# One decoder step: T4's second-level forms from resident parts, the early pairs' sums on VectorE, and block 0 of the hidden layer loaded before its use

## The chip, the cores and the metric

The kernel runs on one core of a Trainium2 chip. The metric is device time in microseconds (us) of that core; lower is better. TensorE (PE in the profile) multiplies matrices, with its weight loads in a row of their own (PEld). VectorE (DVE), ScalarE (ACT) and GpSimd (POOL) do elementwise work, and SyncE (SP) issues most DMAs. Each engine works through its own queue in order; semaphores hold an instruction until what it needs is done.

## The reference, cut to what matters

The program is one layer of a hybrid decoder for 1024 prompt tokens and 8 sample tokens that share the weights: three token mixers (a gated convolution, a state-space scan, cross-attention), their merge, and a SwiGLU feed-forward layer with norms. The change lies in the feed-forward part:

```python
def swiglu(xn, w_gate, w_up, w_down):
    return (jax.nn.silu(xn @ w_gate) * (xn @ w_up)) @ w_down
...
xp = xp + swiglu(rmsnorm(xp, norm_ffn_w[l]), w_ffn_gate[l], w_ffn_up[l], w_ffn_down[l])
```

`xn` has 1032 rows (1024 + 8) of 1024 elements; the hidden size is 2816, that is, 22 blocks of 128.

## The kernel before

**Number format.** Products are made in three passes: every operand is split into a high part (a rounded copy, a cast on ScalarE) and a low part (source minus high part, on VectorE), and hi x hi, hi x lo and lo x hi are summed in PSUM. So every new operand costs one ScalarE and one VectorE instruction ahead of TensorE. `form` (L402, L404) does this for activations, `st_split` (L258, L259) and `w_half` (L2049, L2050) for weights.

**Gate and up projections.** The hidden blocks are worked on in pairs, in the list `pairs`: (0, 9), then eight pairs whose blocks lie four apart, then (10, 19) and (20, 21); n counts them from 0 to 10. For each pair the gate ("g") and then the up ("u") projection is one Strassen product of a 2 x 2 block matrix: seven products of half size with combinations of the activations, the forms B11, T1, nT2, B21, T3, B22 and T4 (names as in `NAMES`), each with its hi and lo part resident. T4's eight parts live in the four tiles of the pool tag `ring`. A name such as u2m or g4c in the profile is the PSUM tile of that projection and block.

For n = 0 to 3, `strassen` runs with the products of B11 and B21 already made (`st_early`); they are fetched from DRAM (`e_d`). Five products are left. Before them, `st_sums` and `st_adds2` combine the two blocks of weights: three sums by `plus` (L296, 128 x 512 each) and one scaled difference (L309) on VectorE. `plus` runs on the engine in `adder`: VectorE at first, GpSimd from n = 1. The first sum is issued behind the instruction in `freed[0]`, where that is on the same engine. VectorE evicts PSUM at L380, L381 (which sets `freed[0]`), L390, L392 and L397, and ScalarE copies at L344 and L379. TensorE accumulates into the same two PSUM tiles again, so it waits for those evictions. The SwiGLU products of a pair follow at L2202 to L2218.

For n = 4 to 10, `chain` makes five of the seven products, and the two others are split once more by a second level of Strassen, `leaf`, whose seven products are interleaved with the next pair's chain: leaf l = 0 for B21 and l = 1 for T4. Pair 4's chain has no leaf work beside it. `leaf_begin` loads and sums a leaf's weights into two `ev` tiles.

**Second-level forms.** `leaf_forms(l)` returns eight functions: `fetch` gets the source (four blocks, two tiles), the others make one second-level form each (four of them with a combination on VectorE at L2024, L2028, L2032 or L2036), split it (L2018 cast, L2019 difference) and store five of the seven through the single tile of the pool tag `stage` into `lf_d`; the last two stay resident. The sources B21 and T4 are stored in `lr_d` when their forms are made (L1862, L1967) and read back by `fetch` (L2008) into two of the five `ev` tiles. Both sets are put into the list `pend` at n = 1; `tick()`, called three times in each early `strassen`, takes one entry. `flush()` empties the list after pair 3. Then `ring_load` begins to bring the stored forms into the four `ring` tiles.

**Down projection.** Part 0 has block 0 by itself and the eight blocks of `PARTS[0]`; the second part has blocks 9 and 10 and eight more. For a block by itself `hidden` loads the SwiGLU result from `h_d` into an `ev` tile and splits it. The 16 halves `pd` (L2337) are its products with the weights; for part 0 the last two leaves (names l010 and l110) are interleaved with the first eight. `hidden_forms` loads the stored combinations of the eight blocks from `hf_d` into `ev` tiles and splits them (names B1100 to T402), and `down_pairs` runs Strassen products d00, d02, d04, d06 with them. In part 0 the first three forms are issued before the `pd` loop, the fourth behind the fourth copy of `pd` results and the others behind the eighth. `begun` prepares the first weights of d00.

**What sets the order.** The code is written once in program order; a scheduler places instructions into each engine's queue by priority in program order and by when it expects operands and buffers to be ready. Where an instruction waits longer on the chip than expected, everything behind it on its queue waits too. `tc.issue_after(x)` puts the instructions of a block that run on x's engine behind x. Pools hold a fixed number of tiles for a tag: 5 `ev`, 8 `big`, 3 raw weight tiles, 12 + 12 for forms, 4 `ring`, 1 `stage`; a load waits until a tile is free.

Of the kernel before, what the change touches and what calls it, by code (L numbers as in the profile page):

```python
# [9 lines left out]
F32 = mybir.dt.float32  # L10
F32R = mybir.dt.float32r
AF = mybir.ActivationFunctionType
ALU = mybir.AluOpType
# [4 lines left out]
P = 128  # L18
# [25 lines left out]
def tile_kernel(ctx: ExitStack, tc, a, o):  # L44
# [3 lines left out]
    def f32(t):  # L48
        return t.bitcast(F32)
# [21 lines left out]
    def dram(name, shape):  # L71
        return dp.tile(shape, F32, tag=name, name=name)
# [100 lines left out]
    def ev_tile(name, shape=(P, TT + 4), dt=F32):  # L173
        return ev.tile(list(shape), dt, tag="ev", name=name)
# [16 lines left out]
    def flush():  # L191
        while pend:
            tick()
# [42 lines left out]
    def b3(t, n):  # L236
        return t.rearrange("p (a b) -> p a b", a=n)
# [181 lines left out]
    h_d = dram("h_d", [NF, P, TT])  # L419
    hf_d = dram("hf_d", [7, 8, P, HT])  # L420
    e_d = dram("e_d", [7, P, TT])
    lr_d = dram("lr_d", [2, 4, P, HT])
    lf_d = dram("lf_d", [2, 5, P, 4, HC])
    q_d = dram("q_d", [8, P, TT])
    k_d = dram("k_d", [2, P, D])
# [1433 lines left out]

    def form_second(kt):  # L1860
        b21 = normed(kt + 4, 0)
        SY.dma_start(lr_d[0, kt], b21)  # L1862
        form("B21", kt, b21)

    for half in range(2):
# [97 lines left out]
    def last_forms():  # L1963
        for kt in range(4):
            t2, b21 = x2[kt][:, HS[0]], x2[kt + 4][:, HS[0]]
            V.scalar_tensor_tensor(t2, t2, -1.0, b21, op0=ALU.mult, op1=ALU.subtract)
            SY.dma_start(lr_d[1, kt], t2)  # L1967
            form("T4", kt, t2, freed[0])

    def hidden_pair(nm, j, j2):  # L1970
# [30 lines left out]
    def leaf_forms(l):  # L2001
        xy = []

        def fetch():
            for i in range(2):
                t = ev_tile(f"lr{l}{i}")
                xy.append(t[:, :TT].rearrange("p (k h c) -> p k h c", k=2, h=2))
                SY.dma_start(b3(t[:, :TT], 2), lr_d[l, 2 * i : 2 * i + 2].rearrange("k p c -> p k c"))  # L2008

        def b(i, j):  # L2010
            return xy[i - 1][:, :, j - 1, :]

        def put(i, src):
            if i < 5:
                t = pstg.tile([P, 4, HC], F32R, tag="stage", name=f"lf{l}{i}")
            else:
                t = leaf_tiles[l, i] = act_tile(("ah", "al")[i % 2], f"lf{l}{i}", shape=(P, 4, HC))
            S.copy(t[:, 0:2, :], src)  # L2018
            V.tensor_sub(t[:, 2:4, :], src, f32(t)[:, 0:2, :])  # L2019
            if i < 5:  # L2020
                SY.dma_start(lf_d[l, i], f32(t))

        def t1():
            V.tensor_sub(b(1, 1), b(1, 2), b(1, 1))  # L2024
            put(1, b(1, 1))

        def t2():
            V.tensor_sub(b(1, 1), b(1, 1), b(2, 2))  # L2028
            put(2, b(1, 1))

        def t3():
            V.tensor_sub(b(1, 2), b(2, 2), b(1, 2))  # L2032
            put(4, b(1, 2))

        def t4():
            V.scalar_tensor_tensor(b(1, 1), b(1, 1), -1.0, b(2, 1), op0=ALU.mult, op1=ALU.subtract)  # L2036
            put(6, b(1, 1))

        return [
            fetch, lambda: put(0, b(1, 1)), t1, t2, lambda: put(3, b(2, 1)), t3, lambda: put(5, b(2, 2)), t4,  # L2040
        ]

# [153 lines left out]

    for n, (j, j2) in enumerate(pairs[:4]):
        if n == 1:
            adder[0] = G
            pend.extend(leaf_forms(0) + leaf_forms(1))  # L2200
        s1, s2, pa = hidden_pair("g", j, j2)
        S.activation(s1, s1, AF.Silu)  # L2202
        S.activation(s2[:, HS[1]], s2[:, HS[1]], AF.Silu)
        S.activation(s2[:, HS[0]], pa, AF.Silu, scale=-1.0)
        u1, u2, pa = hidden_pair("u", j, j2)
        V.tensor_mul(s1, s1, u1)
        V.tensor_mul(s2[:, HS[1]], s2[:, HS[1]], u2[:, HS[1]])
        V.scalar_tensor_tensor(s2[:, HS[0]], pa, -1.0, s2[:, HS[0]], op0=ALU.mult, op1=ALU.mult)
        if j2 != j + 4:
            SY.dma_start(h_d[j], s1)  # L2210
            SY.dma_start(h_d[j2], s2)
            continue
        (b11, b12), (b21, b22) = ([t[:, c] for c in HS] for t in (s1, s2))
        (t1, t3_), (t2, t4) = ([t[:, c] for c in HS] for t in (u1, u2))
        V.tensor_sub(t1, b12, b11)
        V.tensor_sub(t2, t1, b22)
        V.tensor_sub(t3_, b22, b12)
        V.scalar_tensor_tensor(t4, t2, -1.0, b21, op0=ALU.mult, op1=ALU.subtract)  # L2218
        for f, t in enumerate((b11, t1, t2, b21, t3_, b22, t4)):
            store_pair(n, f, t)  # L2220
    flush()
    for _ in range(4):
        ring_load()

# [3 lines left out]
    def leaf_next():  # L2228
        l, n, og, ou, after = jobs.popleft()
        return leaf(l, n, ready.popleft(), og, ou, after)  # L2230

    for n in range(4, len(pairs)):
        j, j2 = pairs[n]
        tiles = []
        for i, nm in enumerate("gu"):
            oo = [big(f"{nm}{j}o{h}") for h in (1, 2)]
            tiles += oo
            side = leaf_next() if n > 4 else iter(())
            for step, _ in enumerate(
                chain(2 * (n - 4) + i, *(wblock(ffn[nm], x * P) for x in (j, j2)), f"{nm}{j}", oo)  # L2240
            ):
                next(side, None)
                if step == 2 and (n > 4 or i):
                    ready.append(leaf_begin(0, n) if i else leaf_begin(1, n - 1))
            for _ in side:
                pass
            s2, u2 = tiles[1], oo[1]
            if i == 0:
                S.activation(s2[:, HS[1]], s2[:, HS[1]], AF.Silu)
            else:  # L2250
                V.tensor_mul(s2[:, HS[1]], s2[:, HS[1]], u2[:, HS[1]])
        s1, s2, u1, u2 = tiles
        done = (n, s1, s2, u1, u2)
        jobs.append((0, n, s1[:, HS[0]], u1[:, HS[0]], lambda done=done: first_done(*done)))
        jobs.append((1, n, s2[:, HS[0]], u2[:, HS[0]], lambda done=done: second_done(*done)))
# [57 lines left out]


    for part, js in enumerate(([0], [9, 10])):
        hl = [hidden(j) for j in js]
        cols = 1024 // len(js)
        rows = a["w_ffn_down"][0, js[0] * P : (js[-1] + 1) * P].rearrange("(k p) c -> p k c", p=P)
        ws = [weights(rows[:, :, c : c + cols], f"wd{js[0]}{c}") for c in range(0, D, cols)]
        fs = {}  # L2320
        hidden_forms(part, fs, NAMES[:3])
        if part:
            begun = st_begin(*down_src(part, 0), f"d{part}0", ev_sums)

        tags = ("m0", "m1", "m2") if count[0] % 2 == 0 else ("m2", "m1", "m0")
        puts = []
        for m in range(KD):
            if not part:
                x2[m] = big(f"x3_{m}")
            for half in range(2):  # L2330
                ps = st_ps(tags[(2 * m + half) % 3], f"pd{part}{m}{half}")
                for k, (ah, al) in enumerate(hl):
                    ks = slice(k * cols + m * P % cols, k * cols + m * P % cols + P)
                    wh, wl = ws[m * P // cols]
                    for i, (wt, x) in enumerate(((wh, ah), (wh, al), (wl, ah))):
                        for po, xc in halves_of(ps, x, half * HT):
                            PE.matmul(po, wt[:, ks], xc, start=(k == 0 and i == 0), stop=(k == len(hl) - 1 and i == 2))  # L2337
                t = x2[m][:, HS[half]]
                if part:
                    V.tensor_tensor(t, hv(ps), t, op=ALU.add)  # L2340
                elif m == 0:
                    V.tensor_copy(t, hv(ps))
                else:
                    puts.append(S.copy(t, hv(ps)).ins)
                if not part and m < 4:
                    if half == 0 and m % 2 == 0:
                        side = leaf_next()
                    next(side, None)
                    if m == 0 and half == 0:
                        ready.append(leaf_begin(1, len(pairs) - 1))  # L2350
                        adder[0] = V
                    if m == 3 and half == 1:
                        begun = st_begin(*down_src(part, 0), f"d{part}0", ev_sums)
        count[0] += 1

        with nullcontext() if part else tc.issue_after(puts[3]):
            hidden_forms(part, fs, NAMES[3:4])
        with nullcontext() if part else tc.issue_after(puts[7]):
            hidden_forms(part, fs, NAMES[4:])
        if not part:  # L2360

            pend.extend([None] * 3 + [lambda m=m: residual(m) for m in range(KD)] + [None])
        down_pairs(part, fs, begun)
        assert not pend
# [170 lines left out]
```

## Time and profile before

| | |
|---|---|
| runs, median of 3 (range) | 2453.87 us (2447.24 to 2456.54) |
| profiled execution | 2450.34 us, span 2448.6 us |
| granted TensorE clock, mean over the span | 0.995 |
| early pairs 0 to 3 (from g0) | about 1783 to 1918 us of the span |
| pairs 4 to 10 (chains and leaves) | about 1918 to 2184 us |
| down projection, part 0 | about 2184 to 2290 us |

The profile comes from one execution. Busy time of an engine counts its instructions, not its waits. In the views of waits a row reads "engine, what it was about to do <- what it waited for: us in total, times, longest us"; in the views of time a row is start, duration, engine, line, operation, written <- read tiles, and in brackets the idle time before and what ended it. L with a number is a line of the kernel.

### The profile page before, as it was taken

To read this page: it belongs to the slowest core of one execution; us is meant where nothing else is said; L and a number is where in the kernel's file an instruction comes from. 1 tells how busy PE (TensorE), PEld (TensorE's weight loads), DVE (VectorE), ACT (ScalarE), POOL (GpSimd) and SP (SyncE) were. 2 spreads that over 40 slices of the span, in tenths; PEclk is the share of its full clock that TensorE was granted. 3 is DMA by queue.
4 is the path that set the end of the run, shared out by engine and by line. 5 is a ranking of instruction groups with operands and counts; after the bars stand their busy time and mean duration, and the time that the engine had idled before them with its cause. 6 is when DMAs were issued, how large, how long until landed. Compare 5 with 4: busy or idle time off the path is not lost. (4 is left out here: it accounts for less than half of the span.)

```text
span 2448.6 us, 45899 instructions
## 1 busy us (share of the span) xinstructions
PE 2397.8 (98%) x18632; PEld 2277.8 (93%) x18632; DVE 1682.3 (69%) x2727; ACT 1118.8 (46%) x1824; POOL 266.6 (11%) x293
## 2 busy tenths in 40 slices
PE   8999999999999999999999999999998999999998
PEld 6999999999999999888888987999998999999998
DVE  6744687767767775568687753645767678777965
ACT  6634555455453544646455442214543344443423
POOL 0000000000000000212211000000022555420000
PEclk9999999999999999999999999999999999999999
DMA  6354433444353446669796887946566699895622
GB/s 214 131 158 154 129 96 119 117 143 138 117 156 113 126 122 198 198 219 299 241 292 211 269 297 245 312 138 192 162 216 208 179 265 275 263 285 185 197 84 82
DMA packets 413371, 461.84 MB, mean 189 GB/s; under 512 B 18415, under 2 KB 329823, under 8 KB 413152
## 3 DMA queue, kind: packets, MB, share of 16 engines
q1 hardware_dynamic: 390022, 395.64, 52.8%
q10 hardware_dynamic: 23137, 63.26, 6.8%
q8 instruction: 147, 2.41, 0.4%
q14 instruction: 65, 0.52, 0.1%
HBM read 335.29 MB, written 123.78 MB: 187 GB/s over the span
## 5 line engine op out<-in xcount | busy, mean ns | idle before, releaser
L1018 ACT ACTIVATE r<-r,acum 128x128 f32<-128x128 f32 x256 | 79.3, 391 | 3.6 <-DMA r<-ac_d 2.7
L1051 POOL TENSOR_TENSOR xdd<-xdt,decst 128x512 f32<-128x512 f32 x32 | 35.2, 1101 | 286.1 <-DVE xdt L1047 280.2
L807 DVE SCALAR_TENSOR_TENSOR ax<-u,prm,ax 128x1024 f32<-128x1024 f32 x44 | 56.4, 1281 | 0.1
L296 POOL TENSOR_TENSOR g1sa<-g1r 128x512 f32<-128x512 f32 x1 | 1.8, 1773 | 489.0 <-DMA g1r<-in_w_ffn_gate_dram 489.0
L959 ACT ACTIVATE st<-st,es 128x128 f32<-128x128 f32 x128 | 41.3, 392 | 22.3 <-DMA st<-in_state_ssm_dram 19.6
L1045 DVE TENSOR_TENSOR r<-r,cbm 128x1024 f32<-128x1024 f32 x32 | 39.1, 1223 | 4.3 <-ACT r L1020 2.4
L1070 DVE TENSOR_TENSOR y<-po,ea 128x512 f32<-128x512 f32 x28 | 19.3, 690 | 33.1 <-PE po L1066 33.1
L961 DVE SCALAR_TENSOR_TENSOR st<-sr,dts,st 128x128 f32<-128x128 f32 x128 | 40.2, 345 | 0.4
L1087 PE MATMUL pss<-xdd,bT 128*128 128x512 f32 x64 | 34.7, 624 | 3.3 <-ACT bT L1044 2.3
L863 POOL MEMSET u<- 128x3 f32 x22 | 2.1, 100 | 326.4 <-PE ps_ex L786 196.0
L1508 DVE TENSOR_TENSOR yr<-po,yr 128x1032 f32<-128x1032 f32 x8 | 9.9, 1232 | 39.5 <-PE po L220 39.4
L965 DVE SCALAR_TENSOR_TENSOR sr<-st,sr 128x128 f32<-128x128 f32 x128 | 35.3, 286 | 1.1
L1074 PE MATMUL py<-r,xdt 128*64 128x128 f32 x512 | 35.0, 279 | 0.0
L1020 ACT ACTIVATE r<-r 128x1024 f32<-128x1024 f32 x32 | 33.9, 1058 | 0.7
L1100 POOL TENSOR_TENSOR s<-s,cdec 128x512 f32<-128x512 f32 x28 | 33.1, 1181 | 1.6 <-DVE s L1093 1.4
L1897 DVE TENSOR_TENSOR x<-pm,xT 128x516 f32<-128x516 f32 x15 | 10.4, 695 | 32.3 <-PE pm L1883 32.3
L1812 DVE TENSOR_TENSOR gt<-po,gt 128x1032 f32<-128x1032 f32 x8 | 9.9, 1232 | 31.5 <-PE po L220 29.6
L1074 PEld LDWEIGHTS py<-r,xdt 128*64 128x64 f32 x512 | 27.3, 136 | 4.4 <-issue 1.0
L1066 PE MATMUL po<-bc,s 128*128 128x128 f32 x224 | 29.6, 275 | 0.0
L1066 PEld LDWEIGHTS po<-bc,s 128*128 128x128 f32 x224 | 28.0, 191 | 1.0
L1623 ACT ACTIVATE pr<-psa,mx 128x256 f32<-128x256 f32 x32 | 14.9, 470 | 30.2 <-DVE mx L1621 30.2
L810 DVE SCALAR_TENSOR_TENSOR ax<-u,prm,ax 128x1032 f32<-128x1032 f32 x22 | 28.3, 1288 | 0.0
(8957 smaller groups left out, 9173.0 us busy)
## 6 DMA issues: line engine op xcount, KB each, us to landing
rg<-lf_d SPq DMA_DIRECT2D x70, 516.0 KB
r<-ac_d SPq DMA_DIRECT2D x32, 512.0 KB
gt_d<-G ACTq DMA_DIRECT2D x24, 516.0 KB
gt<-gt_d SPq DMA_DIRECT2D x24, 516.0 KB
xs_d<-ax ACTq DMA_DIRECT2D x22, 516.0 KB
zs<-zs_d SPq DMA_DIRECT2D x16, 516.0 KB
yb_d<-x SPq DMA_DIRECT2D x16, 516.0 KB
in<-yb_d SPq DMA_DIRECT2D x16, 516.0 KB
```

What stands on the lines that cost most here:

```text
L807: V.scalar_tensor_tensor(acc[:, :T], u[:, j : j + T], w[j], acc[:, :T], op0=ALU.mult, op1=ALU.add)
L959: S.activation(st[:, i], st[:, i], AF.Copy, scale=es[:, g * 4 + i, b : b + 1])
L961: V.scalar_tensor_tensor(st[:, i], rb, dts[:, g * 4 + i, b : b + 1], st[:, i], op0=ALU.mult, op1=ALU.add)
L965: V.scalar_tensor_tensor(rb, st[:, i], 1.0, rc, op0=ALU.mult, op1=ALU.mult, accum_out=ys[:, g * 4 + i, b : b + 1],)
L1018: S.activation(r[:, j, :], r[:, j, :], AF.Relu, scale=-1.0, bias=acum[:, c, h : h + 1])
L1020: S.activation(r, r, AF.Exp, scale=-1.0)
L1045: V.tensor_tensor(r, r, bc(cbm.unsqueeze(1), [P, HPG, P]), op=ALU.mult)
L1051: G.tensor_tensor(b3(xdd, HPG), b3(xdt, HPG), bc(decst[:, c, hs].unsqueeze(2), [P, HPG, 64]), op=ALU.mult)
L1066: PE.matmul(po[:, t * P : (t + 1) * P], state["s"][:, t * P : (t + 1) * P], bcg[1][:, cs], start=True, stop=True,)
L1074: PE.matmul(py[hp : hp + 64, (h // 2) * P : (h // 2 + 1) * P], xdt[:, h * 64 : (h + 1) * 64], r[:, (h % 2) * 4 + h // 2, :], start=True, s ...
L1087: PE.matmul(pss, bT, xdd, start=True, stop=True)
L1100: G.tensor_tensor(b3(s_new, HPG), b3(state["s"], HPG), bc(cdec[:, c, hs].unsqueeze(2), [P, HPG, 64]), op=ALU.mult,)
```

## The change

- The source of T4's second-level forms is no longer stored and read back. `fetch` for l = 1 rebuilds it in two `big` tiles by adding T4's resident high and low parts on VectorE, four additions of 128 x 516.
- `adder` stays on VectorE through pairs 1 to 3 and becomes GpSimd after `flush()`.
- Only the forms of l = 0 go into `pend`, each followed by an empty entry. Those of l = 1 start after `flush()`: `fetch` at once, then one of the others after each step of pair 4's chains.
- The SwiGLU result of block 0 is loaded at the start of pair 9 into the `stage` tile, and only split at the beginning of the down projection.
- For part 0, the first three forms are issued in the second half of m = 2 of the `pd` loop, and what they have on VectorE goes behind the last weight split issued by then.

```diff
@@ leaf_forms
-                t = ev_tile(f"lr{l}{i}")
-                xy.append(t[:, :TT].rearrange("p (k h c) -> p k h c", k=2, h=2))
-                SY.dma_start(b3(t[:, :TT], 2), lr_d[l, 2 * i : 2 * i + 2].rearrange("k p c -> p k c"))
+                t = (big if l else ev_tile)(f"lr{l}{i}")[:, :TT]
+                xy.append(t.rearrange("p (k h c) -> p k h c", k=2, h=2))
+                if l == 0:
+                    SY.dma_start(b3(t, 2), lr_d[2 * i : 2 * i + 2].rearrange("k p c -> p k c"))
+                    continue
+                for k, c in enumerate(HS):
+                    hi, lo = (f32(x) for x in forms["T4"][2 * i + k])
+                    V.tensor_tensor(t[:, c], hi, lo, op=ALU.add)
@@ last_forms
-            SY.dma_start(lr_d[1, kt], t2)
@@ pairs 0 to 3
         if n == 1:
-            adder[0] = G
-            pend.extend(leaf_forms(0) + leaf_forms(1))
+            pend.extend(f for p in leaf_forms(0) for f in (p, None))
...
     flush()
+    adder[0] = G
+    turned_forms = leaf_forms(1)
+    turned_forms[0]()
     for _ in range(4):
         ring_load()
@@ pairs 4 to 10
+    h0 = []
     for n in range(4, len(pairs)):
         j, j2 = pairs[n]
+        if n == len(pairs) - 2:
+            h0.append(pstg.tile([P, 4 * LW], F32, tag="stage", name="h0r")[:, :TT])
+            SY.dma_start(h0[0], h_d[0])
...
                 next(side, None)
+                if n == 4 and len(turned_forms) > 1:
+                    turned_forms.pop(1)()
@@ down projection
-        hl = [hidden(j) for j in js]
+        hl = [split_act(h0[0], "h0")] if part == 0 else [hidden(j) for j in js]
...
-        hidden_forms(part, fs, NAMES[:3])
+        if part:
+            hidden_forms(part, fs, NAMES[:3])
...
+                    if m == 2 and half == 1:
+                        with tc.issue_after(prev["lo"]):
+                            hidden_forms(part, fs, NAMES[:3])
```

More of the change, by code (lines that the diff above doesn't have):

```diff
@@ L421, in tile_kernel @@
     e_d = dram("e_d", [7, P, TT])
-    lr_d = dram("lr_d", [2, 4, P, HT])
+    lr_d = dram("lr_d", [4, P, HT])
     lf_d = dram("lf_d", [2, 5, P, 4, HC])
@@ L1861, in form_second @@
         b21 = normed(kt + 4, 0)
-        SY.dma_start(lr_d[0, kt], b21)
+        SY.dma_start(lr_d[kt], b21)
         form("B21", kt, b21)
```

## The prediction

> **What bounds the kernel now.** I read the page first, then the busy time by stretches, then what TensorE waited for in the stretches that lose time, then the queue of the engine it waited for.
>
> ```profile
> PE 2397.8 (98%) x18632; PEld 2277.8 (93%) x18632; DVE 1682.3 (69%) x2727; ACT 1118.8 (46%) x1824; POOL 266.6 (11%) x293
> ```
>
> TensorE (PE) sets the end. A microsecond is won only where TensorE stops or runs at a lower clock, so I looked for such places among the lines that change. The columns below are: stretch, its length, then busy time and number of instructions for PE, weight loads, VectorE (DVE), ScalarE (ACT), GpSimd (POOL), then the granted clock and the DMA share.
>
> ```profile
> 1785.20:1800.20 15.00, 15.00 (x128) 14.96 (x127) 11.17 (x16) 9.23 (x14) 1.28 (x1) 1.00 0.64 201
> 1800.20:1904.00 103.80, 90.47 (x695) 88.57 (x694) 71.40 (x91) 35.34 (x50) 28.21 (x20) 0.93 0.63 199
> 1904.00:1923.00 19.00, 19.00 (x162) 18.95 (x161) 13.67 (x15) 6.35 (x11) 9.01 (x6) 1.00 0.53 153
> 1923.00:1945.00 22.00, 20.93 (x174) 20.52 (x173) 12.43 (x18) 6.93 (x12) 10.23 (x9) 1.00 0.85 217
> 2157.00:2180.00 23.00, 20.86 (x162) 20.65 (x161) 16.03 (x24) 11.63 (x17) 1.33 (x2) 0.93 0.96 304
> 2180.00:2210.00 30.00, 27.12 (x215) 25.77 (x213) 23.86 (x40) 18.01 (x29) 3.19 (x4) 1.00 0.90 287
> 2210.00:2233.40 23.40, 21.50 (x172) 20.68 (x173) 21.01 (x25) 11.51 (x13) 0.00 (x0) 1.00 0.71 223
> ```
>
> The first row is the first pair undisturbed: 15.00 / 128 = 0.117 us for each matmul. At that pace the 695 matmuls of the second row (the rest of pair 0, pairs 1 to 3 up to u3) need 81.4 us and took 103.8: **22.4 us lost**. The seam into the down projection (last three rows) loses 23.0 - 19.0, 30.0 - 25.2 and 23.4 - 20.2: **12.0 us**. The fifth pair (n = 4, third and fourth row) loses 0 and 1.6 us. These losses are all that the change can win.
>
> What TensorE waited for in the lossy pair stretch:
>
> ```profile
> PE u2m L271 <- DVE u2o L390: 4.1, 1, 4.1
> PE g2m L271 <- DVE g2o L381: 3.1, 1, 3.1
> PE u0m L271 <- DVE u0o L381: 3.0, 1, 3.0
> PE u1m L271 <- ACT u1o L344: 1.3, 1, 1.3
> ...
> PE u1m L271 <- DVE u1o L390: 0.4, 1, 0.4
> ```
>
> The idle time is 103.80 - 90.47 = 13.3 us; the eight waits sum to it. Three long ones make 10.2. The clock row of the same stretch, 0.93, costs another 0.07 x 103.8 = 7.3 us: after each long stop the matmuls run slower for a while. And why VectorE was late with its evictions:
>
> ```profile
> DVE u3sb L309 <- POOL u3sa L296: 5.1, 1, 5.1
> ...
> DVE g1sb L309 <- POOL g1sa L296: 2.6, 1, 2.6
> DVE g2sb L309 <- POOL g2sa L296: 2.4, 1, 2.4
> DVE g3sb L309 <- POOL g3sa L296: 2.4, 1, 2.4
> ...
> DVE u2sb L309 <- POOL u2sa L296: 1.8, 1, 1.8
> ```
>
> VectorE stood 14.3 us waiting for GpSimd's weight sums, with evictions queued behind. The worst case in order of time, VectorE's queue and then GpSimd's:
>
> ```profile
> 1881.12 1.74 DVE L309 SCALAR_TENSOR_TENSOR u3sb<-u3sa,u3r 128x512 f32<-128x512 f32 x1 [5.11 <-POOL u3sa L296]
> 1882.78 0.68 DVE L2019 TENSOR_TENSOR lf<-lr,lf 128x516 fp32r<-128x516 f32 x1
> 1883.38 0.68 DVE L390 TENSOR_TENSOR u2o<-u2o,u2m 128x516 f32<-128x516 f32 x1
> ```
> ```profile
> 1878.45 1.29 POOL L296 TENSOR_TENSOR u3sa<-u3r 128x512 f32<-128x512 f32 x1 [8.23 <-DMA u3r<-in_w_ffn_up_dram]
> ...
> 1881.04 1.26 POOL L296 TENSOR_TENSOR u3sb<-u3r,u3r 128x512 f32<-128x512 f32 x1
> ```
>
> L309 needs u3sa, GpSimd needs the raw weights, and L390, which TensorE waits for, stands two places behind L309. L309 itself took 1.74 us while GpSimd was adding.
>
> **Part 1: sums of pairs 1 to 3 on VectorE.** `adder` stays V until after `flush()`. Eighteen sums (six Strassen steps by three) leave GpSimd. Their price on VectorE is the same line in the input projection:
>
> ```profile
> L296 DVE TENSOR_TENSOR Z2sb<-Z2r,Z2r x1: 692/692/692, 86.5 to 86.5; 128x512 f32<-128x512 f32 x1
> L2018 ACT CAST lf<-lr x14: 603/622/627, 1798.4 to 1884.7; 128x516 fp32r<-128x516 f32 x14
> L2019 DVE TENSOR_TENSOR lf<-lr,lf x14: 681/692/698, 1803.8 to 1885.8; 128x516 fp32r<-128x516 f32 x14
> SPq L2021 <- DVE lf L2019: 31.4, 9, 7.6
> ```
>
> That is 18 x 0.69 = 12.4 us more work. What goes: the second set of leaf forms leaves these pairs, four combinations (L2024 to L2036, taken at the 0.69 of L2019) and seven splits, 11 x 0.69 = 7.6 us, with seven casts of 0.62 = 4.3 us on ScalarE and five of the stores for which SP's queue stood 31.4 us in all; raw weight loads are queued behind those stores. VectorE's work becomes 71.4 + 12.4 - 7.6 = 76.2 us in 81.4 us of matmuls, less the stretching beside GpSimd (1.74 against 0.69, seen on about five instructions, 5 us): 71 to 76, or 87 to 94%. That is dense, but the sums stand behind `freed[0]` (L381 of the step before, which now is on their own engine), so the eviction at L381 goes ahead of them, and the 14.3 us of waits vanish.
>
> What is late next: the waits on ScalarE's copy L344 (1.3 and 0.6) and three of 0.4 stay, 3.1 us. Of g2's 3.1 us I leave half, since the SwiGLU products of the pair before (L2206 to L2218, on VectorE) still stand ahead of its L381. That is 4.7, say 5 us left of 22.4: **-17.4 us**. Bounds: -22.4 (nothing left); above, the third rival's +6.6.
>
> A point on the clock: the row 2157 to 2180 shows 0.93 in a stretch whose only stop on the quoted list is 2.1 us (below), so I reckon a leftover stop of 2 us as also costing clock, and leave no room below 5. [...]
>
> **Part 2: T4's second-level forms in the fifth pair.** Removed: four stores into `lr_d[1]` and two loads, all from SP's queue. Added in pair 4: four adds of hi and lo (L296's 0.69 each), then the same 11 VectorE instructions, seven casts and five stores, now one form after each chain step. VectorE: 15 x 0.69 = 10.4 us into two stretches with 41.0 - 26.1 = 14.9 us free. ScalarE's 4.3 us has 27.7 free. But in this pair no leaf work stands between the chain's steps, so a step's eviction has only 2.84 us of cover (24 matmuls, below); the single `stage` buffer makes each cast wait for the store before it; and SP's loads for the next chain queue behind the stores. Bounds: 0 (all beside matmuls) and 10.4 (all on the path). Since VectorE reaches 26.1 + 10.4 = 36.5 of 41 us (89%), I take a quarter: **+2.5 us**. The T4 forms' buffers, the ring's four tiles, come free four adds (2.8 us) later:
>
> ```profile
> L2060 SPq DMA_DIRECT2D rg<-lf_d x70: 518/524/1167, 1916.9 to 2197.0; - x70
> ```
> ```profile
> 1948.64 2.84 PE g11c L271 x24
> 1951.48 0.71 PE l04pa L2068 x6
> ```
>
> The first ring load went out at 1916.9 and its first reader ran at 1951.5; 2.8 us is hidden by these 34.6. If that were gone, it would be the 2.8.
>
> **Part 3: block 0 and its forms at the seam.** `h0` is loaded before pair 9 ends into the free `stage` tile instead of taking a slot of the five `ev` tiles; and the six loads, six casts and six splits for B11, T1 and nT2 move behind six of the sixteen `pd` halves, the splits behind the last weight split issued then.
>
> ```profile
> PE u20c L271 <- DVE u20o L2155: 2.1, 1, 2.1
> ...
> PE l110pa L2068 <- ACT l110w L2049: 1.3, 1, 1.3
> PE l110pa L2068 <- DVE g20o L2100: 0.7, 1, 0.7
> ```
> ```profile
> POOL l110a L296 <- DMA l110b<-in_w_ffn_up_dram: 34.6, 1, 34.6
> ...
> DVE B1102al L404 <- ACT B1102ah L402: 3.1, 1, 3.1
> ...
> ACT B1102ah L402 <- DMA B<-hf_d: 2.6, 1, 2.6
> ```
> ```profile
> 2186.93 1.23 DVE L404 TENSOR_TENSOR nT202al<-nT,nT202ah 128x1032 fp32r<-128x1032 f32 x1
> ```
>
> TensorE's 2.1 us goes back to VectorE standing at B1102al, that to a cast, that to a load: a form that no product before 2210 reads blocks an eviction. With its clock this is the 4.0 us of the stretch 2157 to 2180. The l110 leaf's weights come late because the forms hold the `ev` slots (2.0 us of stops). Both go: -6.0. Against it: VectorE was busy 23.9 of 30.0 and 21.0 of 23.4 us after 2180. Two splits that ran before 2180 (B11, 2 x 1.23) come to it, and the four other first-level forms (eight loads through the same five slots) follow later. I charge 2.5 us for the two splits and 0.5 for the later loads: **-3 us**. Bounds: -12.0 (nothing lost) and +3.4 (all six splits, 7.4 us, on the path after the leaf's last weight split, less the 4.0). The 0.5 MB of `h0` in pair 9 I cost at nothing: every chain stretch there is covered by matmuls; without that cover it is one load.
>
> **The sum.** 2450.34 us for the profiled execution (span 2448.6 and 1.7 around it, unchanged): 2450.3 - 17.4 + 2.5 - 3.0 = 2432.4. The median of the runs, 2453.87, lies 3.5 above the profiled execution, so I forecast **2436**. Its own range is 2429 to 2442.
>
> **Rivals.**
>
> *The weights' loads are the wait, not GpSimd.* The POOL row above itself waited for u3r, which landed at 1878.45. On VectorE the same wait blocks evictions directly: four instructions at 0.6 us after that landing put L390 at about 1880.9 instead of 1883.4, so 4.1 becomes 1.6 us. With 1.6 us in each of six steps, 9.6, and clock for half of them (3 x 1.6), 14 of the 22 us stay: -8 + 2.5 - 3, or 2445. For it: the 8.2 us wait. Against: five fewer stores ahead of the loads, buffers freed earlier by quicker sums, and L381 ahead of the sums.
>
> *The seam becomes bound by VectorE.* All six splits land on the path: +3.4 instead of -3; with the fifth pair at 5 instead of 2.5 that gives 2445 as well, and 2449 if pairs win only 13. For it: 21.0 of 23.4 us. Against: TensorE has next products to put ahead, as VectorE at 90% there cost only 3.2 us.
>
> *Slower: VectorE cannot be filled.* If VectorE's share cannot rise over the 69% (71.4 / 103.8) of the pairs, 76.2 us of work take 110.4 us, 6.6 more than now; and the fifth pair's 36.5 us at the 74% of the clean first row take 49.3, 8.3 more. That is +15: 2469. It decides from the point where VectorE stays under 74%. For it: queue order is fixed and strict. Against: the row 2210 to 2233 shows 90%. [...] At 69% this trace does not show saturation.
>
> *The seam clears fully* and the pairs keep only 2 us of stops: -20.4 + 0 - 8 = 2425.
>
> *It does not act:* the waits stay, shifted to other instructions, with 2454. The five waits have a named cause that is gone, so little.
>
> **Chances.** Forecast 0.55; loads 0.15; seam 0.10; slower 0.06; full 0.09; no effect 0.05. The range reaches to 2425 below and 2450 above, taking in all but the slower and no-effect cases and edges. A change under 0.5% (12.3 us) can't be told from none here; the line lies at 2441.6. Faster: most of the forecast (0.50), the full case (0.09), and some of loads and seam (0.07): 0.66. Slower: 0.06. The rest, 0.28, is within.
>
> **What would show it.** Right: no wait of VectorE on GpSimd in pairs 1 to 3, clock 1.00 and about 86 us for the 695 matmuls; VectorE above 80% there; in pair 4 stops of 2 to 3 us after L2155 or L2159; no stop at u20c; the l110 loads ahead of the B11 loads. Wrong: VectorE waiting for raw weights at the new sums (first rival); stops of d00 on the first splits (second); a clock below 1.00 in pair 4 or in the pairs (third).

## The result and the profile after

| | before | changed |
|---|---|---|
| median of the runs (range) | 2450.73 us, 7 runs (2445.36 to 2456.54) | 2439.31 us, 7 runs (2434.09 to 2444.06) |
| profiled execution | 2450.34 us, span 2448.6 | 2436.37 us, span 2434.6 |

The changed kernel takes 0.995 of the time, with a 95% interval of 0.9933 to 0.9967: 11.4 us less. The forecast was 2436 in a range of 2425 to 2450.

To place the 14 us between the two profiled executions I cut both spans at the same products, each at the row in TensorE's timeline where the product starts (start, duration, engine, line, operation, operands). In the changed kernel these rows are:

```profile
1781.45 0.40 PE L271 MATMUL g0m<-T10h,g0Sh 128*128 128x256 f32 x2
...
1882.06 0.41 PE L271 MATMUL u3m<-T10h,u3Sh 128*128 128x256 f32 x2
...
1933.17 0.40 PE L271 MATMUL g11c<-B110h,g11A 128*128 128x256 f32 x2
...
2145.31 0.40 PE L271 MATMUL u20c<-B110h,u20A 128*128 128x256 f32 x2
...
2220.52 0.40 PE L271 MATMUL d02m<-T100ah,d02Sh 128*128 128x256 f32 x2
```

| stretch | before | changed | difference |
|---|---|---|---|
| start to g0m | 1783.5 | 1781.5 | -2.1 |
| **pairs**: g0m to u3m | 120.4 | 100.6 | -19.8 |
| **fifth pair**: u3m to g11c | 44.5 | 51.1 | +6.6 |
| g11c to u20c | 212.1 | 212.1 | 0 |
| **seam**: u20c to d02m | 75.2 | 75.2 | 0 |
| d02m to the end | 212.8 | 214.1 | +1.3 |

Up to g0m the code differs only by T4's four stores, and that stretch varies from 1780.0 to 1787.1 us over all the runs below, with or without them, so its -2.1 tells nothing. The pairs win more than forecast, the fifth pair costs more, and the seam, where something was taken away and something came back, is worth nothing. The busy time by stretches shows how (columns as in the prediction). First the kernel before, with the same matmuls as the first two rows after it:

```profile
1796.90:1904.00 107.10, 93.77 (x723) 91.87 (x722) 73.83 (x94) 37.95 (x55) 29.49 (x20) 0.94 0.62 196
1904.00:1948.50 44.50, 43.44 (x363) 42.97 (x362) 27.78 (x35) 14.49 (x25) 22.66 (x19) 1.00 0.69 184
```

The changed kernel: the pairs, the fifth pair, the chain of u4 in it, and three pieces of the seam (to the first `pd` product, to d00, and d00):

```profile
1794.80:1882.00 87.20, 86.71 (x722) 86.19 (x721) 72.83 (x101) 33.90 (x47) 0.96 (x1) 1.00 0.63 198
1882.00:1933.20 51.20, 46.26 (x363) 44.85 (x363) 41.91 (x50) 18.10 (x32) 30.38 (x22) 0.97 0.74 212
1913.90:1933.10 19.20, 16.59 (x122) 15.96 (x122) 13.36 (x14) 7.79 (x14) 16.39 (x14) 0.91 0.80 238
2145.30:2164.60 19.30, 19.30 (x164) 19.30 (x163) 13.35 (x23) 9.39 (x14) 3.58 (x4) 1.00 0.90 273
2164.60:2191.40 26.80, 22.61 (x182) 21.81 (x181) 22.81 (x37) 17.33 (x27) 0.00 (x0) 1.00 0.93 306
2191.40:2217.60 26.20, 21.80 (x170) 21.48 (x169) 21.95 (x26) 12.44 (x14) 0.00 (x0) 0.93 0.72 240
```

In the pairs TensorE now idles 0.5 us (87.20 - 86.71) instead of 13.3, at a clock of 1.00 instead of 0.94. VectorE is busy for 72.83 of 87.20 us, 84%.

In the fifth pair TensorE idles 4.9 us, the clock is 0.97, and VectorE's work has grown by 14.1 us (27.78 to 41.91) for 15 more instructions. What TensorE waited for there (engine, line; what it waited for; us in total, times, longest):

```profile
PE u4c L271 <- DVE u4o L2159: 2.3, 1, 2.3
PE g4c L271 <- DVE g4o L2159: 0.7, 1, 0.7
PE g4c L271 <- ACT g4o L2151: 0.6, 1, 0.6
```

And VectorE's timeline up to the eviction that ends the 2.3 us:

```profile
1920.97 1.78 DVE L2054 TENSOR_TENSOR l04w<-l04a,l04w 128x512 fp32r<-128x512 f32 x1
1922.73 1.72 DVE L2023 TENSOR_TENSOR lf<-lr,lf 128x516 fp32r<-128x516 f32 x1
1924.37 1.75 DVE L2054 TENSOR_TENSOR g11S<-g11sa,g11S 128x512 fp32r<-128x512 f32 x1
1926.03 0.68 DVE L2159 TENSOR_TENSOR u4o<-u4c,u4o 128x516 f32<-128x516 f32 x1
```

Three differences of two inputs from SBUF, a kind that takes 0.67 to 0.70 us in the changed kernel's rows that no GpSimd instruction overlaps, take 1.7 to 1.8 here, where GpSimd is adding block weights (16.39 us of the 19.20). The one of a form (L2023) is one of them, and the eviction stands behind it.

At the seam the stop at u20c is gone (the 19.3 us up to the first `pd` product are all matmul, 23.2 before), but d00 stops:

```profile
PE d00m L271 <- ACT d00Th L258: 4.4, 1, 4.4
PE pd L2350 <- ACT x L2357: 1.6, 2, 1.4
PE l010pa L2072 <- DMA rg<-lf_d: 1.6, 1, 1.6
PE l110pa L2072 <- DMA rg<-lf_d: 0.9, 1, 0.9
```

d00Th is the cast of T's weights for d00, made from d00sb. VectorE's timeline ahead of it:

```profile
2202.65 1.23 DVE L404 TENSOR_TENSOR T400al<-T,T400ah 128x1032 fp32r<-128x1032 f32 x1
2203.80 0.68 DVE L296 TENSOR_TENSOR d00sb<-d00r,d00r 128x512 f32<-128x512 f32 x1
2204.46 1.23 DVE L404 TENSOR_TENSOR T402al<-T,T402ah 128x1032 fp32r<-128x1032 f32 x1
2205.61 0.68 DVE L309 SCALAR_TENSOR_TENSOR d00sb<-d00sa,d00r 128x512 f32<-128x512 f32 x1
2207.40 1.23 DVE L259 TENSOR_TENSOR d00Tl<-d00sb,d00Th 128x1024 fp32r<-128x1024 f32 x1 [0.51 <-ACT d00Th L258]
```

The second half of d00's weights (L296, L309) stands behind form splits (L404), among them those of T4, the last product that d00 uses. So the six splits moved later push the eight others onto d00's weights. The waits on l110's weights and evictions (1.3 and 0.7 us before) are gone as foreseen; that leaf now waits for its stored forms instead (0.9), and so does l010 (1.6).

### The profile page after: what moved, and what is told of

It reads as the page before. It is cut to its first block, busy times and chain, and to the rows that moved or that the text cites. A ratio compares the mean times of both kernels' runs of the same rounds, so it can differ in the third digit from the quotient of the medians.

```text
span 2434.6 us, 45868 instructions
## 1 busy us (share of the span) xinstructions
PE 2390.9 (98%) x18632; PEld 2272.4 (93%) x18632; DVE 1694.0 (70%) x2749; ACT 1119.1 (46%) x1824; POOL 244.4 (10%) x275
## 4 chain that ended last, share of the span: by engine, by line
PE 84%; DMA 7%; DVE 6%; ACT 2%; issue 1%; SPq 0%; DVEq 0%; ACTq 0%
PE po L220 11%; PE pm L1883 4%; PE ps_q L220 3%; PE py L1074 1%; PE pss L1087 1%; PE ps_z L220 1%; PE po L1066 1%; PE G16m L271 1%; PE d14m L271 1%; PE Z2m L271 1%; PE Z14m L271 1%; PE Z12m L271 1%; PE Z8m L271 1%; PE Z10m L271 1%; PE Z6m L271 1%
## 5 line engine op out<-in xcount | busy, mean ns | idle before, releaser
L296 POOL TENSOR_TENSOR g4sa<-g4r 128x512 f32<-128x512 f32 x1 | 2.1, 2062 | 572.5 <-DMA g4r<-in_w_ffn_gate_dram 572.5
L1070 DVE TENSOR_TENSOR y<-po,ea 128x512 f32<-128x512 f32 x28 | 19.3, 690 | 31.9 <-PE po L1066 31.9
L1897 DVE TENSOR_TENSOR x<-pm,xT 128x516 f32<-128x516 f32 x15 | 10.4, 695 | 32.3 <-PE pm L1883 32.3
```

## The experiments

Stretches are in us of each kernel's profiled execution, cut as above. "Base" is the kernel that was edited.

| kernel | base | pairs | fifth pair | seam | time, and ratio to before |
|---|---|---|---|---|---|
| before | | 120.4 | 44.5 | 75.2 | |
| changed | | 100.6 | 51.1 | 75.2 | 0.995 (0.9933 to 0.9967) |
| e1_sums_only | before | 102.0 | 43.4 | 75.2 | 2433.17, 0.9923 (0.9904 to 0.9941) |
| e2_forms_only | before | 119.3 | 49.6 | 74.5 | 2453.33, 1.001 (0.9998 to 1.0022) |
| e3_pairs_only | changed | 100.9 | 51.2 | 75.5 | 2437.29, 0.9938 (0.9918 to 0.9958) |
| e4_seam_only | before | 122.2 | 44.5 | 78.4 | 2451.28, 1.0003 (0.9991 to 1.0014) |
| e5_ev_stage | changed | 100.8 | 49.7 | 75.8 | one run, 2433.27 |
| e6_pair4_sums_V | changed | 101.7 | 49.0 | 76.8 | one run, 2436.69 |
| e9_no_edge | changed | 111.0 | 50.3 | 77.5 | one run, 2452.05 |
| e12_source_from_dram | changed | 100.4 | 49.0 | 76.2 | one run, 2435.3 |
| e15_all_three | changed | 101.1 | 50.0 | 76.5 | one run, 2441.37 |
| e10_sums_seam | before | 103.9 | 43.4 | 75.8 | 2430.71, 0.9921 (0.9906 to 0.9936) |
| e14_sums_t_old_seam | before | 103.0 | 43.4 | 69.9 | 2429.55, 0.9919 (0.9903 to 0.9936) |
| e11_sums_seam_t | before | 104.6 | 43.4 | 70.8 | 2429.31, 0.9899 (0.9882 to 0.9915) |

The kernel before took 2449.8 to 2454.7 us beside these runs, so the times of different rows compare to a few us, the ratios and stretches more closely. Each stretch comes from one execution. With the same code in it, the fifth pair repeats to 0.1 us (43.4 four times, 51.1 and 51.2); the pairs vary from 102.0 to 104.6 (e1, e14, e10, e11) and from 120.4 to 122.2 (before, e4). The seam takes 74.5 to 75.5 us in the four kernels with the old code and 75.2 to 78.4 in the eight with the changed code. Differences of that size tell nothing. The profiled execution of e4 is the slowest of its ten, 2458.39.

### The parts one by one

The sums alone, without moving any form:

```diff
         if n == 1:
-            adder[0] = G
             pend.extend(leaf_forms(0) + leaf_forms(1))
...
     flush()
+    adder[0] = G
```

> The kernel before with one part of the change: the sums of pairs 1 to 3 run on VectorE; both sets of second-level forms stay in the pairs. Theory A (VectorE stood behind GpSimd's sums): the stretch from g0's first T1 product to u3's, 120.4 us before and 100.6 after the change, falls to between 103 and 110, with no wait of VectorE on GpSimd; it can't reach 100.6, since VectorE's work there is 71.4 + 12.4 = 83.8 us less some 5 of stretching beside GpSimd, against 81.4 of matmuls. The kernel gets 8 to 14 us faster. Rival B (the stores and casts of the second set of forms held the loads up): the stretch stays within 5 us of 120.4.

The forms of T4 moved and rebuilt, sums as before (the changed kernel without its seam part, and with this):

```diff
         if n == 1:
+            adder[0] = G
             pend.extend(f for p in leaf_forms(0) for f in (p, None))
```

> The change's forms part alone: T4's second-level forms in the fifth pair, sums of pairs 1 to 3 on GpSimd as before, the seam as before. Theory A: the stretch from g0's to u3's T1 product stays at 112 us or more of 120.4, VectorE still waits 8 us or more on GpSimd; with 5 us or more lost in the fifth pair the kernel is no faster than before. Rival B: the stretch falls to 106 or less, and the kernel gains what the change gains, about 11 us.

Both, without the seam part (the lines with `h0` and the late `hidden_forms` undone); then the seam part alone:

> The change without its seam part (block 0 and the first three forms of the down projection as before). If the seam part is worth nothing, as the two traces say (from u20's first product to d02's: 72.8 us before, 72.4 after), this runs within 2 us of the changed kernel, about 2439, and the stretch from g0 to u3 takes 100.6. If the seam part is worth the 3 us forecast, this is 3 us slower than the changed kernel. If it costs, hidden by something else, this is faster.

> The kernel before with the seam part alone. Theory (VectorE bounds the seam): the stop at u20c goes, 3 to 4 us are won up to the first pd product, and are given back before d02, as d00's T weights wait for VectorE behind eight splits of forms; the kernel stays within 2 us of before. Forecast of the prediction: 3 us faster. Rival (the splits land on the path and cost more than the stop): 3 us slower.

**Measured.** The sums alone win 18.4 of the 19.8 us of the pairs, 102.0 where 103 to 110 was expected; the forms alone win 1.1 there, less than the same code varies, and cost 5.0 in the fifth pair, so alone they bring nothing (1.001). That the forms crowded VectorE was thus not why evictions came late. In e2, with fewer forms in the pairs, VectorE waits for GpSimd as before and longer:

```profile
DVE u3sb L309 <- POOL u3sa L296: 6.0, 1, 6.0
DVE u2sb L309 <- POOL u2sa L296: 5.9, 1, 5.9
...
DVE g3sb L309 <- POOL g3sa L296: 4.2, 1, 4.2
DVE g1sb L309 <- POOL g1sa L296: 2.6, 1, 2.6
DVE g2sb L309 <- POOL g2sa L296: 2.4, 1, 2.4
```

e1's pairs and fifth pair, in the busy time by stretches:

```profile
1798.20:1886.80 88.60, 87.05 (x723) 86.21 (x722) 78.60 (x112) 37.54 (x55) 0.00 (x0) 1.00 0.75 237
1886.80:1930.20 43.40, 43.25 (x363) 42.95 (x362) 27.63 (x36) 14.52 (x25) 25.98 (x20) 1.00 0.69 189
```

With all the forms still in the pairs VectorE is busy for 78.60 of 88.60 us, 89%, and TensorE loses 1.6 us. The fifth pair runs at its full pace, 43.4. So moving the forms buys 1.4 us in the pairs (102.0 - 100.6; 2.4 between the means of the four kernels with all forms there, 103.4, and of the six like the changed one, 100.9) and costs 7.7 in the fifth pair (51.1 - 43.4). The sums' move takes away two things at once, VectorE's waits for GpSimd and the stretching of its instructions beside it (83.27 us for 108 instructions in the 120.4 us before, 87.92 for 126 in e1's 102.0: 0.77 and 0.70 us each). These runs do not split the 18.4 us between them; the next experiment shows what waits alone can do. e3's pairs and fifth pair are those of the changed kernel; its seam is the old one and costs the same (the 72.8 and 72.4 us in its expectation are counted to an earlier product of d02 than the T1 product used in this document). e4's seam, 78.4, is no better either, with the same wait at d00:

```profile
PE d00m L271 <- ACT d00Th L258: 4.3, 1, 4.3
```

### Are the raw weights the wait that was held off?

The first of a step's sums waits for its raw weights, and on VectorE it would block evictions meanwhile. In the kernel it is issued behind the eviction in `freed[0]`. This kernel takes that order away:

```diff
-        with nullcontext() if behind is None else tc.issue_after(behind):
+        with nullcontext():
             plus(sa[:, :512], raw2[:, :512], raw2[:, 512:])
```

> The changed kernel without the order that puts the first sum behind the eviction at L381 of the step before. If that order is what keeps the waits for raw weights off VectorE's evictions, VectorE waits on the loads (in1 to 3 us a piece) and the stretch from g0 to u3, 100.6 us, grows to 104 to 112. If the loads are early enough anyway, it stays within 1.5 of 100.6, and the rival of the loads had no ground.

**Measured.** The pairs take 111.0 instead of 100.6 us. The longest waits of VectorE, and then of TensorE, in them:

```profile
DVE u3sa L296 <- DMA u3r<-in_w_ffn_up_dram: 3.7, 1, 3.7
DVE u2sa L296 <- DMA u2r<-in_w_ffn_up_dram: 3.0, 1, 3.0
DVE u1sa L296 <- DMA u1r<-in_w_ffn_up_dram: 2.9, 1, 2.9
```
```profile
PE u1m L271 <- DVE u1o L381: 3.5, 1, 3.5
PE u2m L271 <- DVE u2o L381: 2.9, 1, 2.9
```

GpSimd works for only 2.83 us in that stretch, so here VectorE's waits, not the stretching, make TensorE late. The first rival was thus a real mechanism, and the order behind L381 is what keeps it out. That rival left 9.4 us more than the forecast in the pairs (-8 instead of -17.4); without the order it is 10.4.

### What the fifth pair pays for

Three suspects: the single `stage` tile, each cast waiting for the store before it (e5); the two engines side by side (e6); the four additions and their place on VectorE (e12, where the source is stored in `lr_d[1]` and loaded again). Then all three edits together (e15).

```diff
@@ e5: leaf_forms
-                t = pstg.tile([P, 4, HC], F32R, tag="stage", name=f"lf{l}{i}")
+                t = ev_tile(f"lf{l}{i}", (P, 4, HC), F32R) if l else pstg.tile([P, 4, HC], F32R, tag="stage", name=f"lf{l}{i}")
@@ e6
     flush()
-    adder[0] = G
...
     for n in range(4, len(pairs)):
         j, j2 = pairs[n]
+        if n == 5:
+            adder[0] = G
@@ e12: leaf_forms
-                if l == 0:
-                    SY.dma_start(b3(t, 2), lr_d[2 * i : 2 * i + 2].rearrange("k p c -> p k c"))
-                    continue
-                for k, c in enumerate(HS):
...
+                SY.dma_start(b3(t, 2), lr_d[l, 2 * i : 2 * i + 2].rearrange("k p c -> p k c"))
```

> The changed kernel, but T4's second-level forms pass through free ev tiles instead of the single stage tile on their way to DRAM. The fifth pair (from u3's T1 product to the chain of block 11) takes 51.1 us in the changed kernel, 44.5 before and 43.4 with the sums alone. If the cost is ScalarE waiting for the store before (9.5 us in four waits), it falls to 44 to 47. If it is VectorE's work (41.9 us busy, against 27.8 before), it stays at 49 to 51.

> The changed kernel with the weight sums of the fifth pair on VectorE too; GpSimd takes them from the sixth on. If VectorE's instructions cost so much there because they are stretched beside GpSimd's sums (1.2 to 1.8 us instead of 0.7), the fifth pair falls from 51.1 us to 46 to 48, and VectorE has no instruction of 128 x 516 over 1 us there. If VectorE's work itself is the cost, the eight more sums (5.5 us) leave it at 51 or lift it to 55.

> The changed kernel, but T4's source is stored and read back as before instead of rebuilt by four additions; its forms stay in the fifth pair. If the four additions (2.8 us of VectorE) are a good part of the fifth pair's 51.1 us, it falls to 48 to 49.5. If the cost is the eleven instructions, seven casts and five stores of the forms, it stays at 50 to 52, and rebuilding from resident parts is worth nothing either way.

> The changed kernel with all three edits of the fifth pair at once: block sums on VectorE there, the forms' stage in five buffers, T4's source stored and loaded instead of four additions. One by one they won 2.1, 1.4 and 2.1 us of the fifth pair's 51.1 (49.0, 49.7, 49.0). Theory that each removes a cause of its own: the stretch from u3's last products to g11 comes to about 51.1 - 5.6 = 45.5 us (44.5 to 46.5), and the time about 2430. Rival, that all three shorten the same late chain step and something else still blocks it: 48.5 to 49.5 us, and TensorE again has one stop of about 2 us in the chain of u4 or g4. If the sums on VectorE make it too full once the stops are gone, above 46.5 with several stops of under 1 us.

**Measured.** The stretch falls from 51.1 to 49.7, 49.0 and 49.0 us, never to 43.4, and little of that is shown to come from the edits. The fifth pair in e5, e6 and e12, in the busy time by stretches:

```profile
1880.82:1930.56 49.74, 45.66 (x363) 44.63 (x361) 40.02 (x49) 18.24 (x32) 24.08 (x18) 0.97 0.69 215
1883.61:1932.57 48.96, 44.28 (x362) 43.17 (x361) 40.74 (x62) 18.42 (x32) 10.50 (x9) 1.00 0.81 222
1883.25:1932.29 49.04, 44.18 (x362) 43.13 (x361) 38.77 (x46) 18.29 (x32) 28.25 (x21) 1.00 0.84 243
```

TensorE idles 4.9 us in the changed kernel and 4.1, 4.7 and 4.9 us here. What e6 and e12 win is mostly clock: 1.00 against 0.97, which is 1.7 us, and the last section has equal stops of 2.3 us in the changed kernel and e12, one with that cost and one without. So by the idle time the stage tile (e5) costs up to 0.9 us, and the additions (e12) and the two engines side by side (e6) next to nothing by themselves; e6's 49.0 lies between its two expected ranges and speaks for neither. The stretching is real: in e6, where GpSimd works for only 10.50 us, VectorE does 62 instructions in 48.96 us where the changed kernel does 50 in 51.1, 0.66 us each instead of 0.84. It buys little; VectorE now has the sums to do as well and is as busy as before (40.74 us against 41.9). With all three edits the stretch is 50.0 us, not the 45.5 of gains that add up; TensorE idles 4.9 us again, with a new wait. TensorE, VectorE and SP's queue in e15:

```profile
PE u4c L271 <- DVE u4o L2155: 3.7, 1, 3.7
```
```profile
DVE l04a L296 <- DMA l04b<-in_w_ffn_up_dram: 6.8, 1, 6.8
```
```profile
SPq L2082 <- DMA lf_d<-lf: 4.8, 1, 4.8
```

The leaf's weights (l04) are loaded into `ev` tiles; those now hold forms that wait for their stores, so SP's queue stands 4.8 us, the weights come late, VectorE waits 6.8 us for them at a sum, and the eviction that u4 needs is behind it. In the changed kernel these weights come 2.4 us after u4's chain begins, in e15 8.9 us, and there it is GpSimd that stood before its first sum for l04, with no eviction behind it:

```profile
POOL l04a L296 <- DMA l04b<-in_w_ffn_up_dram: 6.8, 1, 6.8
```

So the cost changes its place with the arrangement: stretched instructions with the sums on GpSimd, a wait for weights with the sums on VectorE and the forms in `ev` tiles. Only leaving the forms in the pairs (e1) removes the cost. How the 7.7 us split between the stage tile, stretching, the forms' own work and clock is not settled by these runs.

### The seam, crossed with T's weights ahead

If d00's stop comes from its own weights standing behind the form splits, preparing them ahead of the splits should remove it, with or without the seam part. `begun` then also makes T's weights for d00:

```diff
@@ strassen
-            raw1, raw2, sa, wA, wS = begun
+            raw1, raw2, sa, wA, wS, *wT = begun
+            if wT:
+                ready = raw1, raw2, sa, wS, wT[0]
...
             raw1, raw2, sa, wS, wT = ready
+            if begun is not None:
+                put(o11, pa)
@@ down projection
                         begun = st_begin(*down_src(part, 0), f"d{part}0", ev_sums)
+                        begun += (st_sums2(*begun[:3], f"d{part}0", ev_sums),)
```

e10 is e1 with the seam part, e14 is e1 with T's weights ahead, e11 has both.

> The kernel before with the sums of pairs 1 to 3 on VectorE and the change's seam part, d00's T weights as before. If the seam part is worth nothing by itself, u20's first product to d02's T1 takes 75 to 78 us, and the kernel the 2433 of the sums alone, within 3 us. If it wins where no forms in the fifth pair press on it, it takes 72 or less.

> The kernel before with the sums of pairs 1 to 3 on VectorE and d00's T weights split early; the seam otherwise as before. If the T weights alone bring the seam's 4 us, u20's first product to d02's T1 takes 70 to 72 us here too (75.2 with the sums alone, 70.8 with the seam part and the T weights), and the change's seam part is not needed. If they need each other, as the stop at u20c (4 us with its clock) stays here, it takes 73 to 76.

> The kernel before with the sums of pairs 1 to 3 on VectorE, the seam part of the change, and d00's T weights summed and split along with its other first weights, ahead of the later forms. Theory (the seam's win is given back where d00 waits 4.4 us for its T weights, which stand behind eight form splits on VectorE): the stop at d00Th goes, the time from u20's first product to d02's T1, 75.2 us before and after the change, falls to between 68 and 72, and the kernel is 3 to 6 us faster than with the sums alone (2433), the lowest so far. If VectorE's whole work bounds the seam, another stop takes its place and it stays at 74 to 76.

**Measured.** The seam stretch, on top of the same sums:

| | T's weights as before | T's weights ahead |
|---|---|---|
| old seam | 75.2 (e1) | 69.9 (e14) |
| seam part of the change | 75.8 (e10) | 70.8 (e11) |

T's weights ahead win 5.3 and 5.0 us; the seam part costs 0.6 and 0.9, less than the stretch varies. Of the 5.3 us in the first row, 2.2 lie before the first `pd` product (23.3 us in e1, 21.1 in e14): the stop at u20c is 1.5 us there instead of 2.2, and the clock 1.00 instead of 0.93. e2, without T's weights ahead, has 21.2 there too, so these 2.2 us are not shown to come from them, and 3.1 remain. In e10 the d00 stop is 3.6 us; in e14 d00Tl is made before 2195, and no stop of TensorE in d00 is left:

```profile
2193.11 1.22 DVE L259 TENSOR_TENSOR d00Tl<-d00sb,d00Th 128x1024 fp32r<-128x1024 f32 x1
```

e11 and e14 are the fastest of the study, 24.8 and 20.3 us under the kernel before beside them; their intervals overlap, so which of the two is better stays open. e14's interval (0.9903 to 0.9936) also takes in the ratios of e1 and e10, so what T's weights win on the old seam shows in the stretch alone, not in the whole time. Both beat the changed kernel, whose interval (0.9933 to 0.9967) lies wholly above e11's and overlaps e14's only from 0.9933 to 0.9936.

## Why the prediction was right, and where its steps were not

The sum ended 4.0 us too low for the profiled execution (2432.4 against 2436.4), from errors of both signs: pairs -2.4, fifth pair +4.1, seam +3.0, the rest -0.8 (-2.1 and +1.3), which makes 3.9. That these partly cancel is luck; the largest term had the right mechanism.

**Part 1, the pairs: right, 2.4 us too small.** -17.4 was forecast, -19.8 measured. That the sums' move brings it and the forms' move doesn't is shown by e1 and e2; that evictions behind VectorE's waits can cost such an amount, 10.4 us there, is shown by e9. VectorE waits for GpSimd nowhere in the changed kernel's pairs, the clock is 1.00, and 722 matmuls take 86.7 us. The mis-sized term is the leftover of 5 us: the changed kernel idles 0.5. VectorE's work came to the lower end of the forecast: 73.8 in the row of before with the same 722 matmuls, + 12.4 - 7.6 - 5 is 73.6, and it was 72.8, 84% of the stretch. That the forms had to leave to make room is refuted by e1: with VectorE at 89% the pairs take only 1.4 us more.

**Part 2, the fifth pair: right direction, wrong size.** +2.5 was forecast, +6.6 measured, inside the bounds of 0 and 10.4. Two steps of it fell. The 15 instructions were priced at the 0.69 us of an undisturbed row and took 14.1 us, 0.94 each, although GpSimd's work in that stretch was in the row of before (9.01 and 10.23 us) and the stretching was in the quoted L309. And "a quarter" assumed spare time that could be used anywhere; with 2.84 us of cover for a step's eviction, a form's two instructions at up to 1.8 us each don't fit in. The forecast's sign, stops after this line in pair 4, came as the 2.3 us at u4c, which also cost 1.7 us of clock.

**Part 3, the seam: wrong.** -3 was forecast, 0 measured. What it removes was right: the stretch from u20c to the first `pd` product lost 3.9 us (23.2 to 19.3; forecast 4.0). The 2.0 us of l110's stops did not come back, since the leaves now wait for stored forms (0.9 and 1.6). What the part gives back was put at 3.0 for two splits and later loads; the runs showed 3.9 after the first `pd` product (0.7 up to d00, 3.2 in d00), through a place that the step didn't look at: the later splits stand ahead of d00's own weights. The step priced VectorE's time, and the place in its queue is what decided. e10 and e4 agree: with the old fifth pair and with sums on either engine the part is worth nothing, and if anything costs a little (75.2 to 78.4 us with it, 74.5 to 75.5 without).

**The rivals.** *Loads are the wait* named a true mechanism, which e9 brings out at 10.4 us, and the reason given against it (L381 ahead of the sums) is the one that held. It returned in e15, where nothing orders the sums behind an eviction. *The seam bound by VectorE*: near it, at 0 instead of +3.4, by order rather than by load. *VectorE cannot be filled*: refuted, 84% in the changed kernel and 89% in e1. Moving work back from GpSimd to a VectorE that was 69% busy won 18 us of 120. *No effect* is out by the interval; *the seam clears fully* comes about in part, -5.3 of its -8, and only with T's weights ahead (e14), 2.2 us of it through a shorter stop that is not shown to be their work.

**The chances.** 0.66 for a gain above 0.5%; the measured gain is 0.5% (interval 0.33 to 0.67%), on the line itself. Over seven runs the median of before is 2450.73, 0.4 above its profiled execution; the 3.5 us added in the sum belonged to the three runs shown. The changed kernel's median lies 2.9 above its profiled execution, which is why the medians differ by 11.4 us and the profiled executions by 14.0.

**The clock.** A stop of 2 us "as also costing clock" was right in size (1.6 us by the row 2157 to 2180, 0.07 x 23.0; 1.7 measured at u4c) and half right in kind, since not every such stop costs it; the last section has the numbers. The first rival adds the same 1.6 us for half of its six stops of 1.6 us (3 x 1.6). No run shows that term; at stops of about that length the rows show no loss: e12 stopped 1.7 us at g4c, and its fifth pair reads 1.00; e14 stopped 1.5 us at u20c, and reads 1.00 there.

## What to carry to other kernels

When one engine's result stands at the head of another engine's strict queue, ask what is queued behind the wait: here the sums on a GpSimd that was mostly idle (29.49 us busy of 107.10) cost 18.4 us more than the same sums on a VectorE that was already 69% busy, provided the sums were ordered behind the eviction that the matmuls need; without that order the pairs took 10.4 us more. Where work is moved to a place with free engine time, ask whether its instructions fit between two evictions: the forms cost 7.7 us in the fifth pair. And ask what the moved work lands ahead of: the splits went ahead of d00's first weights, and the 3.9 us won up to the first `pd` product came back behind it. Test the parts alone: one of three carried the whole gain here, and without the other two the pairs and the fifth pair together took 145.4 us instead of 151.7.

## What the runs showed that was not expected

**A stop of about 2 us came with 1.7 us of clock in one execution and with none in another.** At the same product, u4c, the changed kernel stopped 2.3 us and ran that chain at 0.91 (row 1913.90 to 1933.10 above); e12 stopped as long and ran it at 1.00:

```profile
PE u4c L271 <- DVE u4o L2155: 2.3, 1, 2.3
```
```profile
1915.00:1932.30 17.30, 14.85 (x123) 14.43 (x122) 13.43 (x14) 7.78 (x14) 15.03 (x13) 1.00 0.90 261
```

The two chains differ by 1.9 us (19.2 and 17.3) for equal stops. At u20c a stop of 2.2 us went with 0.93 (e1), one of 1.5 with 1.00 (e14).

Two short stretches of the changed kernel, the first with the stop at u4c in it and the second right behind, show where the loss lies:

```profile
1924.01:1927.42 3.41, 1.10 (x9) 0.90 (x9) 3.41 (x4) 0.21 (x1) 3.41 (x3) 1.00 0.57 196
1927.42:1930.84 3.42, 3.42 (x18) 3.42 (x18) 1.22 (x2) 0.62 (x1) 3.34 (x4) 0.50 0.70 243
```

In the first TensorE idles 2.3 us (3.41 - 1.10); in the second it never idles, but the clock is 0.50, which costs half of 3.42 us, 1.7. The kernel before has four such places: the clock reads 0.50 for 3.41 us from 1807.87, 1859.07 and 2176.51 us, next to the stops of 3.0 us at u0m, 3.1 at g2m and 2.1 at u20c, and for 6.82 us from 1882.96, around the end of the 4.1 us at u2m. The stop of 2.1 us is the one from which the prediction had read such a cost. Why the 2.3 us at u4c cost clock in the changed kernel and not in e12 was not shown.

**VectorE's instructions stretched beside GpSimd by up to 2.6 times**, 0.68 to 1.79 us in the changed kernel's fifth pair, where both read two inputs from SBUF; six evictions with one input from PSUM (L397, L2159, L2163, L2168) ran beside GpSimd there and took 0.68 to 0.70 us. The seven form differences in the fifth pair averaged this much (group by line: output and input, count; busy us, mean ns; idle before them):

```profile
L2023 DVE TENSOR_TENSOR lf<-lr,lf 128x516 fp32r<-128x516 f32 x7 | 7.6, 1090 | 2.8 <-ACT lf L2022 2.8
```

against 692 in the prediction's row for the same line. The busy share counts this stretching as work: VectorE's 82% here (41.91 of 51.20) are 50 instructions, and in e6's row 83% (40.74 of 48.96) are 62.
